# A Griffin-style layer in fp32: u, gelu, q and k by seven half-size products too, the recurrent branch spread over them, attention moved beside the recurrent projection

## The chip, the cores and the metric

One core of one Trainium2 chip runs the whole program. The metric is device time in microseconds of one execution; the median of 3 runs before is 1458.74 us (1458.58 to 1458.85).

## The reference, cut to what matters

The layer works on 1024 tokens of width 1024 in fp32. One input projection gives seven parts of each token; an attention branch and a recurrent branch use them and meet before the output projection, then a feed-forward block follows.

```python
h = rms_norm(x, ln1_g)
z = h @ w_in + b_in
q, k, v, u, y, g_att, g_rec = split(z)      # widths 512 512 512 1024 1024 1024 1024
y_att = neighbourhood_attention(q, k, v, rpb) @ w_att_o
u = centred_depthwise_conv(u, conv_w, conv_b)
h_fwd = rg_lru(u, ..., reverse=False)       # two sigmoid gates, then a scan along the tokens
h_bwd = rg_lru(u, ..., reverse=True)
y_rec = ((h_fwd + h_bwd) * gelu(y)) @ w_rec_o
x = x + (sigmoid(g_att) * y_att + sigmoid(g_rec) * y_rec) @ w_out
x = x + square(relu(rms_norm(x, ln2_g) @ w_ff1)) @ w_ff2
return rms_norm(x, lnf_g)
```

## The kernel before, in words

Every fp32 operand of a matrix product is split into a high and a low part of type fp32r, and a product is three matmuls: high by high, high by low, low by high. A matmul takes a 128x128 block of weights and 512 columns (tokens).

The program is written once as a list of operations and ordered by a planner. `M(fn)` (line 379) puts a unit of usually six matmuls on TensorE's main list; `SD(pos, fn, boost)` (line 383) puts side work, on any engine, at a position counted in such units; `here()` is the current position. `Plan.add` (line 119) gives each operation a cost in ns and its predecessors, `Plan.solve` (line 204) runs a list schedule with these costs and a limited number of tile slots and banks, and `Plan.issue` (line 326) records the instructions in the order of the planned start times. So every instruction of the profile has line L332, and groups are told apart by tile names. Engines run their own instructions strictly in that order. For VectorE (DVE) the cost of an operation without a branch of its own is n/0.96+68 ns for n elements a row, the scan among them: 1135 ns at 1024. PSUM tiles carry the tag "pm" (two of them) or "pa" (four).

The stages, with their times in the trace:

- 0 to 76 us: norm, transposes, the v part; 76 to 218 us: the 2048 gate columns in eight **pairs** (`pairs`, line 634).
- 218 to 404 us: q and k as full products (`tprod`, line 815: 48 matmuls for 128 output columns of weights), with the 64 attention tiles (`a_qk`, `a_norm`, `a_tr`, `a_av`, lines 904 to 943) beside them.
- 404 to 613 us: u and y, eight full products each (`utask`, `ytask`, lines 977 to 988), with the recurrent branch of each of eight channel blocks as side work: convolution (tile uc), split (uh, ul), four gate products on TensorE (`gate_pe`), sigmoids, tanh, exp, square and square root (tiles g, th, sq), two scans (`scan`, line 1074).
- 613 to 658 us: projection of the attention result; 658 to 745 us: projection of the recurrent result (both `tprod`); 745 to 839 us: output projection.
- 839 to 1145 us: first feed-forward product, sixteen pairs by the same `pairs`; 1145 to 1457 us: second feed-forward product.

A pair computes two 128-column blocks of weights against the two token halves by seven half-size products of 12 matmuls each (named A11, A12, A22 and S1 to S4 for the weight side), 84 matmuls in place of 96. `pjob` (line 534) loads both weight tiles (ws), makes sums (sa, sb) on DVE and splits them (wh, wl; sh, sl; wx) on ScalarE (ACT) and DVE. `prod` (line 587) runs one product into a bank of its own, and `ev1` to `ev7` (lines 605 to 632) add the seven results together: one ACT copy and seven DVE additions of 128x512 from PSUM. `gate_store` (line 802) applies the sigmoid and stores the gate in DRAM (gd).

Of the kernel before, what the change touches and what calls it, by code (L numbers as in the profile page):

```python
# [4 lines left out]
F32 = mybir.dt.float32  # L5
# [5 lines left out]
P = 128  # L11
# [3 lines left out]
DH = 64  # L15
# [4 lines left out]
NSLOT = 51  # L20
# [86 lines left out]
class Plan:  # L107
# [11 lines left out]
    def add(self, eng, meth, args, kw):  # L119
# [224 lines left out]
def emit(tc, x, prm, wst, wv, wg, watt, wrec, wout, wff1, wff2, tb, bv, lnf, out):  # L344
# [3 lines left out]
    plan = Plan({"t": NSLOT - NW, "w": NW, "s": 48, "pm": 2, "pa": 4, "c": 64, "d": 72})  # L348
    pe, act, dve, pool, sp = [plan.engine(e) for e in ("pe", "act", "dve", "pool", "sp")]

    with ExitStack() as ctx:
# [182 lines left out]
        def pjob(o, srcs, p0, p1):  # L534
# [15 lines left out]
            def sa():  # L550
                o.sa = T("sa", F32, (P, 8, P))
                dve.tensor_add(o.sa[:, 0:4], o.w1[:, 0:4], o.w1[:, 4:8])
                dve.tensor_sub(o.sa[:, 4:8], o.sa[:, 0:4], o.w0[:, 0:4])

            def sb():
                o.sb = T("sb", F32, (P, 8, P))
                dve.tensor_sub(o.sb[:, 0:4], o.w0[:, 0:4], o.w1[:, 0:4])
                dve.tensor_sub(o.sb[:, 4:8], o.w0[:, 4:8], o.sa[:, 4:8])
# [17 lines left out]
            SD(p1 - 20, lambda: dma(1))  # L576
            SD(p1 - 6.8, sa, 6.0)
            SD(p1 - 6.7, lambda: sp_("sa", "ha", "la"), 6.0)
            SD(p1 - 3.2, sb, 6.0)
            SD(p1 - 1.5, lambda: sp_("sb", "hb", "lb"), 6.0)  # L580
            SD(p1 - 0.5, a22, 6.0)
            o.lhs = {"A11": lambda: (o.h0[:, 0:4], o.l0[:, 0:4]), "A12": lambda: (o.h0[:, 4:8], o.l0[:, 4:8]),
                     "S1": lambda: (o.ha[:, 0:4], o.la[:, 0:4]), "S2": lambda: (o.ha[:, 4:8], o.la[:, 4:8]),
                     "S3": lambda: (o.hb[:, 0:4], o.lb[:, 0:4]), "S4": lambda: (o.hb[:, 4:8], o.lb[:, 4:8]),
                     "A22": lambda: (o.a4[:, 0:4], o.a4[:, 4:8])}

        def prod(o, a, ob, b, bank, ev, boost=5.0):

            h = Obj()
            for kk in range(2):  # L590
                def run(kk=kk):
                    if kk == 0:
                        h.ps = VT(nm("pm"), (P, 512), F32, "pm") if bank else PA()
                    hi, lo = o.lhs[a]()
                    for k in (2 * kk, 2 * kk + 1):
                        bh, bl = ob[b]["h"][kk][:, k % 2, :], ob[b]["l"][kk][:, k % 2, :]
                        pe.matmul(h.ps, hi[:, k, :], bh, start=(k == 0), stop=False)
                        pe.matmul(h.ps, hi[:, k, :], bl, start=False, stop=False)
                        pe.matmul(h.ps, lo[:, k, :], bh, start=False, stop=(k == 3))
                last = M(run)  # L600
            SD(last + 0.1, lambda: ev(o, h.ps), boost)

        lft, rgt = slice(0, 512), slice(512, 1024)

        def ev1(o, ps):
            o.r1 = T("r1")
            act.activation(o.r1[:, lft], ps, AF.Copy)

        def ev2(o, ps):
            if o.r0 is None:  # L610
                o.r0 = T("r0")
            dve.tensor_add(o.r0[:, lft], ps, o.r1[:, lft])

        def ev6(o, ps):
            if o.r0 is None:
                o.r0 = T("r0")
            dve.tensor_add(o.r0[:, rgt], ps, o.r1[:, lft])

        def ev7(o, ps):
            dve.tensor_add(o.r1[:, rgt], ps, o.r0[:, rgt])  # L620

        def ev4(o, ps):
            dve.tensor_add(o.r1[:, lft], ps, o.r1[:, rgt])

        def ev5(o, ps):
            dve.tensor_add(o.r0[:, rgt], ps, o.r0[:, rgt])
            dve.tensor_add(o.r1[:, rgt], ps, o.r1[:, rgt])
            o.store(o.r1, 1)

        def ev3(o, ps):  # L630
            dve.tensor_add(o.r0[:, rgt], ps, o.r0[:, rgt])
            o.store(o.r0, 0)

        def pairs(srcs, stores, ob, pre):

            ps_ = []
            for st in stores:
                o = Obj()
                o.r0, o.store = None, st
                ps_.append(o)  # L640
# [3 lines left out]
            for i0 in range(0, pre, 2):  # L644
                g = ps_[i0:min(i0 + 2, pre)]
                for o in g:
                    prod(o, "A11", ob, "B11", 1, ev1, 30.0)
                for o in g:
                    prod(o, "A12", ob, "B21", 1, ev2, 30.0)
            for i, o in enumerate(ps_):  # L650
                if i >= pre:
                    pjob(o, srcs[i], here(), here() + 2)
                    prod(o, "A11", ob, "B11", 1, ev1, 10.0)
                prod(o, "S2", ob, "T2", 0, ev6)
                if i >= pre:
                    prod(o, "A12", ob, "B21", 1, ev2)
                prod(o, "S3", ob, "T3", 0, ev7)
                prod(o, "A22", ob, "T4", 0, ev4)
                prod(o, "S1", ob, "T1", 0, ev5)
                prod(o, "S4", ob, "B22", 0, ev3)  # L660
# [130 lines left out]
        V = [[None, None] for _ in range(4)]  # L791

        def gather_v(g):
            for b in range(2):
                V[g][b] = T("V", F32, (P, 2, 512))
            for b in range(2):
                sp.dma_start(V[g][b], vd[g][2 * b:2 * b + 2].rearrange("n p f -> p n f"))


        gd = [None] * 16  # L800

        def gate_store(i):
            def store(r, half):
                c = 2 * i + half
                act.activation(r, r, AF.Sigmoid, bias=col("bga" if c < 8 else "bgr", c % 8), scale=1.0)
                gd[c] = Dr("gd")
                sp.dma_start(gd[c], r)
            return store

        pairs([(wst[24 + 2 * i], wst[25 + 2 * i]) for i in range(8)], [gate_store(i) for i in range(8)], ob1, PRE1)  # L810
        for g in range(4):
            SD(here() - 4 + 3 * g, lambda g=g: gather_v(g))
# [24 lines left out]
        qs, kh, kl = [None] * 4, [None] * 4, [None] * 4  # L837
        QL, KL = (5.0, 7.0), (0.2, 1.4)
        att, attd = [None] * 4, [None] * 4
        kend = []  # L840
        for m in range(4):
            w = wjob(wst[m], (P, 8, P), here())
            o = tprod(w, hT)

            qs[m] = [None, None]

            def evq(m=m, o=o):
                o.t = T("q")
                for hf in range(2):
                    c = slice(hf * 512, (hf + 1) * 512)  # L850
                    act.activation(o.t[:, c].rearrange("p (n r c) -> p r n c", r=8, c=16),
                                   o.ps[:, c].rearrange("p (r n c) -> p r n c", n=4, c=16),
                                   AF.Identity, bias=bq8[:, m:m + 1], scale=0.125)

            def stq(hd, m=m, o=o):
                qs[m][hd] = t = T("qs", F32R)
                a, b = slice(hd * DH, (hd + 1) * DH), slice((1 - hd) * DH, (2 - hd) * DH)
                act.activation(t[a], o.t[a], AF.Copy)
                dve.tensor_sub(t[b], o.t[a], t[a])
            SD(o.last + 0.1, evq, 30.0)  # L860
            for hd in range(2):
                SD(o.last + QL[hd], lambda hd=hd, f=stq: f(hd))
            w = wjob(wst[4 + m], (P, 8, P), here())
            o = tprod(w, hT)
            kh[m], kl[m] = [None, None], [None, None]

            def evk(m=m, o=o):
                o.t = T("k")
                act.activation(o.t, o.ps, AF.Identity, bias=col("bk", m), scale=1.0)

            def stk(hd, m=m, o=o):
                kh[m][hd] = h = T("kh", F32R)
                kl[m][hd] = l = T("kl", F32R)
                a, b = slice(hd * DH, (hd + 1) * DH), slice((1 - hd) * DH, (2 - hd) * DH)
                act.activation(h[a], o.t[a], AF.Copy)
                act.activation(h[b], o.t[a], AF.Copy)
                dve.tensor_sub(l[a], o.t[a], h[a])
                dve.tensor_sub(l[b], o.t[a], h[a])
            SD(o.last + 0.1, evk, 30.0)
            for hd in range(2):  # L880
                SD(o.last + KL[hd], lambda hd=hd, f=stk: f(hd))
            kend.append(o.last)
        SD(kend[0] - 12, softplus)

# [711 lines left out]
```

## Time and profile before

| what | value |
|---|---|
| median of 3 runs | 1458.74 us |
| profiled execution, its own time | 1459.04 us |
| its span, first to last instruction | 1457.3 us |
| instructions | 17684 |
| PE, DVE, ACT busy | 1434.7, 1061.3, 739.1 us |
| granted TensorE clock | 0.999 |
| HBM traffic | 133 GB/s over the span |

The span leaves 1.74 us of the profiled execution around it. A busy share is that of an engine's instructions over the whole span. Rows give a start (timeline and chain) or a sum and a mean (groups); a start-to-start distance on one engine is up to 0.1 us shorter than the durations, since an instruction begins while the one before ends.

### The profile page before, as it was taken

What the parts mean: (1) busy time and instruction counts of PE and PEld (TensorE: products, weight loads), DVE (VectorE), ACT (ScalarE), POOL (GpSimd) and SP (SyncE); (2) the same over time, 40 slices, a digit from 0 to 9 for tenths busy, and PEclk for the clock granted to TensorE, in tenths of its full rate; (3) what the DMA queues carried; (4) which work ended last, traced back from release to release, by engine and by line L of the source; (5) the groups of instructions that cost most, each with busy time, mean ns of one, the idle gap of its engine ahead of it and who ended that gap; (6) DMA issues with size and microseconds to landing.
All of it is one profiled execution on the core that took longest, in us unless ns stands there. A gap on an engine that the chain in (4) does not pass through costs nothing.

```text
span 1457.3 us, 17684 instructions
## 1 busy us (share of the span) xinstructions
PE 1434.7 (98%) x6688; PEld 1178.1 (81%) x6688; DVE 1061.3 (73%) x1601; ACT 739.1 (51%) x1146; POOL 0.7 (0%) x6
## 2 busy tenths in 40 slices
PE   6999999999999999999999999999999999999997
PEld 5888888778778887888888888888888888888886
DVE  6985645666859899975444589776766976866996
ACT  7743325665576987941225545444443643432454
POOL 0000000000000000000000000000000000000000
PEclk9999999999999999999999999999999999999999
DMA  6532235233311013422323325544446884336312
GB/s 226 150 119 101 102 136 209 94 127 113 109 39 63 30 52 108 156 94 98 130 86 116 122 95 185 175 147 142 152 152 234 311 318 148 113 115 235 117 43 101
DMA packets 71445, 195.47 MB, mean 134 GB/s; under 512 B 7360, under 2 KB 7488, under 8 KB 71360
## 3 DMA queue, kind: packets, MB, share of 16 engines
q1 hardware_dynamic: 71360, 194.35, 38.8%
q8 instruction: 52, 0.85, 0.2%
q14 instruction: 33, 0.27, 0.1%
HBM read 141.89 MB, written 52.43 MB: 133 GB/s over the span
## 4 chain that ended last, share of the span: by engine, by line
PE 88%; DVE 8%; issue 1%; ACT 1%; DMA 1%; SPq 0%; DVEq 0%
PE pa L332 57%; PE pm L332 32%; DVE g L332 3%; DVE wl L332 1%; DVE uc L332 1%; DVE wh L332 1%; DVE y L332 1%; DMA x<-in_x_dram 0%; DVE th L332 0%; ACT h L332 0%; DMA ws<-in_wst_dram 0%; DVE al L332 0%; ACT L332 0%; DVE uh L332 0%; DVE h L332 0%
## 5 line engine op out<-in xcount | busy, mean ns | idle before, releaser
L332 PE MATMUL pa<-wh,rh 128*128 128x512 f32 x448 | 173.9, 389 | 0.0
L332 PE MATMUL pa<-wl,rh 128*128 128x512 f32 x448 | 173.5, 389 | 0.0
L332 PE MATMUL pa<-wh,rl 128*128 128x512 f32 x448 | 172.8, 389 | 0.0
L332 DVE TENSOR_TENSOR r<-pa,r 128x512 f32<-128x512 f32 x144 | 96.9, 688 | 77.0 <-PE pa L332 76.6
L332 PE MATMUL pm<-hTh,wh 128*128 128x512 f32 x448 | 148.5, 399 | 0.0
L332 PE MATMUL pm<-hTl,wh 128*128 128x512 f32 x448 | 146.1, 392 | 0.0
L332 PE MATMUL pm<-hTh,wl 128*128 128x512 f32 x448 | 144.5, 390 | 0.0
L332 DVE TENSOR_TENSOR wl<-ws,wh 128x1024 fp32r<-128x1024 f32 x76 | 92.4, 1221 | 20.5 <-PE pm L332 12.8
L332 ACT ACTIVATE wh<-ws 128x1024 fp32r<-128x1024 f32 x49 | 51.4, 1057 | 105.6 <-DMA ws<-in_wff_dram 58.2
L332 ACT ACTIVATE wh<-w 128x1024 fp32r<-128x1024 f32 x56 | 58.9, 1051 | 88.0 <-PE pa L332 77.8
L332 PEld LDWEIGHTS pm<-hTh,wl 128*128 128x128 f32 x448 | 84.0, 188 | 17.7
L332 PEld LDWEIGHTS pa<-wl,rh 128*128 128x128 f32 x448 | 84.1, 188 | 17.6
L332 PEld LDWEIGHTS pa<-wh,rh 128*128 128x128 f32 x448 | 84.1, 188 | 17.5
L332 PEld LDWEIGHTS pa<-wh,rl 128*128 128x128 f32 x448 | 84.1, 188 | 17.4
L332 PEld LDWEIGHTS pm<-hTl,wh 128*128 128x128 f32 x448 | 83.7, 188 | 17.8 <-issue 0.7
L332 ACT ACTIVATE r<-r 128x1024 f32<-128x1024 f32 x64 | 67.0, 1059 | 59.4 <-DVE r L332 58.9
L332 PEld LDWEIGHTS pm<-hTh,wh 128*128 128x128 f32 x448 | 81.0, 188 | 18.2 <-issue 4.1
L332 ACT ACTIVATE rh<-rs 128x1024 fp32r<-128x1024 f32 x56 | 58.7, 1049 | 42.7 <-DVE wl L332 17.3
L332 DVE TENSOR_TENSOR acc<-pa,acc 128x512 f32<-128x512 f32 x72 | 49.3, 688 | 41.3 <-PE pa L332 41.1
L332 DVE TENSOR_TENSOR wl<-w,wh 128x1024 fp32r<-128x1024 f32 x56 | 68.2, 1219 | 10.6 <-ACT wh L332 9.6
L332 DVE TENSOR_TENSOR rl<-rs,rh 128x1024 fp32r<-128x1024 f32 x56 | 68.2, 1219 | 8.8 <-ACT rh L332 7.9
L332 PE MATMUL pa<-T4h,wx 128*128 128x512 f32 x192 | 63.0, 389 | 0.0
(205 smaller groups left out, 3217.6 us busy)
## 6 DMA issues: line engine op xcount, KB each, us to landing
rs<-rd SPq DMA_DIRECT2D x56, 512.0 KB, 7.2
ws<-in_wst_dram SPq DMA_DIRECT2D x41, 512.0 KB, 4.5
ws<-in_wff_dram SPq DMA_DIRECT2D x36, 512.0 KB, 5.1
w<-in_wff_dram SPq DMA_DIRECT2D x32, 512.0 KB, 6.8
B<-in_tb_dram SPq DMA_DIRECT2D x32, 384.0 KB, 3.7
x<-in_x_dram SPq DMA_DIRECT2D x16, 512.0 KB, 6.4
gd<-r SPq DMA_DIRECT2D x16, 512.0 KB, 2.9
g<-gd SPq DMA_DIRECT2D x16, 512.0 KB, 4.5
```

The source lines that it names most:

```text
L332: getattr(eng[op.eng], op.meth)(*[r(a) for a in op.args], **{k: r(a) for k, a in op.kw.items()})
```

## The change: what it does

- u, y, q and k go through `pairs` as well: with the gates there are 20 pairs in one stretch, in the order of the table PORD.
- The products of a pair are chained in PSUM: A11, S2, S3 and A22 add up in one bank (tag pm), S1 and S4 in another, A12 has its own. Partial sums are read out between (ev1, ev6, ev5 and ev4 as ACT copies; ev2, ev7 and ev3 as DVE additions): four ACT copies and three DVE additions.
- The weight sums are made in place in the ws tiles; weights are loaded 16 and 15 units ahead instead of 22 and 20.
- The recurrent branch hangs on the ends of the u pairs (RSTEP 28, RRATE 1.6). y, q, k, the recurrent result and its projection go through DRAM (yd, qd, kd, recd, yrd).
- The recurrent projection comes before the attention projection, with the attention tiles beside it (AOFF 3, ASTEP 0.8). V is gathered per pair of heads.
- The sigmoid of the 2048 gates becomes 0.5(1+tanh(z/2)), taken beside the two projections, with the factor 0.5 in `wo_ev`.
- The first operation of the convolution, the split of uc and high parts of weights move from DVE to ACT.
- The planner's costs for TensorE change; three tile slots more (51 to 54), with a smaller DMA scratch.

```diff
-NSLOT = 51
+NSLOT = 54
...
-            op.cost = (n * 0.84 if meth == "transpose" else (52 if wr[0].box[0][0] else n * 1.68) if f32 else n * 0.417) + 2.6
+            op.cost = n * 0.84 + 2.6 if meth == "transpose" else (12 if wr[0].box[0][0] else n * 1.68 + 40) if f32 else n * 0.417 + 13.3
...
+            def sums():
+                a, b = o.w0, o.w1
+                o.a4 = VT(nm("wx"), (P, 8, P), F32R, "w")
+                act.activation(o.a4[:, 0:4], b[:, 4:8], AF.Copy)
+                dve.tensor_sub(o.a4[:, 4:8], b[:, 4:8], o.a4[:, 0:4])
+                dve.tensor_add(b[:, 4:8], b[:, 0:4], b[:, 4:8])
+                dve.tensor_sub(b[:, 0:4], a[:, 0:4], b[:, 0:4])
+                dve.tensor_sub(a[:, 0:4], b[:, 4:8], a[:, 0:4])
+                dve.tensor_sub(a[:, 4:8], a[:, 4:8], a[:, 0:4])
...
-            SD(p0 - 22, lambda: dma(0))
+            SD(p0 - 16, lambda: dma(0))
...
-        def prod(o, a, ob, b, bank, ev, boost=5.0):
+        def prod(o, a, ob, b, key, bank, first, ev, boost=5.0):
...
-                    if kk == 0:
-                        h.ps = VT(nm("pm"), (P, 512), F32, "pm") if bank else PA()
+                    if kk == 0 and first:
+                        o.ps[key] = VT(nm("pm"), (P, 512), F32, "pm") if bank else PA()
...
+                    prod(o, "A11", ob, "B11", 0, True, True, ev1, 10.0)
+                    prod(o, "A12", ob, "B21", 1, False, True, ev2)
+                prod(o, "S2", ob, "T2", 0, False, False, ev6)
+                prod(o, "S1", ob, "T1", 2, False, True, ev5)
+                prod(o, "S3", ob, "T3", 0, False, False, ev7)
+                prod(o, "S4", ob, "B22", 2, False, False, ev3)
+                prod(o, "A22", ob, "T4", 0, False, False, ev4)
...
+        PORD = (("u", 0), ("y", 0), ("g", 0), ("u", 1), ("y", 1), ("g", 1), ("g", 2), ("u", 2), ("y", 2), ("g", 3),
+                ("g", 4), ("u", 3), ("y", 3), ("g", 5), ("g", 6), ("g", 7), ("qk", 0), ("qk", 1), ("qk", 2), ("qk", 3))
...
+        RSTEP, RRATE, AOFF, ASTEP = 28.0, 1.6, 3.0, 0.8
...
+            base = end_of["u", j // 2] + 0.3 + (j % 2) * RSTEP
...
+        pos0 = [RO + AOFF + 16 * ASTEP * m for m in range(4)]
...
-            dve.tensor_add(x1[t][:, cs], o.ps, x1[t][:, cs])
+            dve.scalar_tensor_tensor(x1[t][:, cs], o.ps, 0.5, x1[t][:, cs], ALU.mult, ALU.add)
```

How the rows of the programs change at the places of which the prediction speaks (a number behind a name tells tiles of that name apart; a SCALAR_TENSOR_TENSOR g<-g,g is a scan):

On DVE before, in the recurrent stretch, two scans of one channel block stand together, behind them the weight parts of the next products:

```order
L332 TENSOR_TENSOR g_917_4384<-g_917_4384,th_927_4436 128x1024
L332 TENSOR_TENSOR g_925_4426<-g_925_4426,th_929_4446 128x1024
L332 SCALAR_TENSOR_TENSOR g_917_4384<-g_914_4355,g_917_4384 128x1024
L332 SCALAR_TENSOR_TENSOR g_925_4426<-g_922_4410,g_925_4426 128x1024
L332 TENSOR_TENSOR g_947_4543<-g_947_4543,uc_935_4381 128x1024
L332 TENSOR_TENSOR wl_958_4564<-ws_943_4491,wh_956_4514 128x1024
```

On DVE in the change, at the first such place in the stretch of pairs, the two scans stand between the addition that reads bank pa_281 (ev3 of a pair) and the low parts of the weights of the next pairs (wl, sl):

```order
L332 TENSOR_TENSOR r0_270_1595<-pa_281_1657,r0_270_1595 128x512
L332 TENSOR_TENSOR g_257_1522<-g_257_1522,th_271_1585 128x1024
L332 TENSOR_TENSOR g_267_1568<-g_267_1568,th_272_1606 128x1024
L332 SCALAR_TENSOR_TENSOR g_257_1522<-g_251_1481,g_257_1522 128x1024
L332 TENSOR_TENSOR sl_297_1774<-ws_258_1535,sh_296_1761 128x1024
L332 SCALAR_TENSOR_TENSOR g_267_1568<-g_261_1548,g_267_1568 128x1024
L332 TENSOR_TENSOR g_295_1780<-g_295_1780,uc_268_1556 128x1024
L332 TENSOR_TENSOR wl_313_1800<-ws_300_1754,wh_312_1789 128x1024
```

So eviction, scans and weight parts of a pair share one queue within a few instructions; TensorE issues 32 matmuls between the last one into pa_281 and the first that reads wl_313.

On ACT in the change, late in the stretch, the copies out of PSUM stand among the splits and the recurrent block's functions; bank pm_573 is read three times, each time with more products added up in it:

```order
L332 ACTIVATE r0_576_3436<-pm_573_3413 128x512
L332 ACTIVATE wh_579_3441<-ws_568_3403 128x1024
L332 ACTIVATE sq_578_3448<-g_560_3363 128x1024
L332 ACT_TABLE_LOAD
L332 ACTIVATE th_566_3385<-th_566_3385 128x1024
L332 ACTIVATE wx_585_3469<-ws_575_3432 128x512
L332 ACTIVATE th_567_3393<-th_567_3393 128x1024
L332 ACTIVATE r0_576_3436<-pm_573_3413 128x512
L332 ACTIVATE r1_583_3495<-pa_582_3477 128x512
L332 ACTIVATE sh_591_3509<-ws_575_3432 128x1024
L332 ACTIVATE sh_586_3528<-ws_568_3403 128x1024
L332 ACTIVATE r1_583_3495<-pm_573_3413 128x512
```

Before, ACT read one bank of a pair once, and TensorE never added to a bank after it was read.

## Rows read from the trace of the kernel before

**Rows 1.** The page: busy time and share by engine; the chain that ended last, by engine.
```profile
PE 1434.7 (98%) x6688; PEld 1178.1 (81%) x6688; DVE 1061.3 (73%) x1601; ACT 739.1 (51%) x1146; POOL 0.7 (0%) x6
PE 88%; DVE 8%; issue 1%; ACT 1%; DMA 1%; SPq 0%; DVEq 0%
```
**Rows 2.** Chain of waits, pieces: start us, length us, engine, tile, instructions.
```profile
103.64 2.72 PE pm L332 x12
106.36 2.72 PE pa L332 x12
...
1134.42 315.57 PE pa L332 x1392
```
**Rows 3.** Busy time by stage: length; PE, PEld, DVE, ACT, POOL; clock; DMA share; GB/s.
```profile
76.00:218.00 142.00, 142.00 (x628) 117.60 (x628) 86.20 (x120) 48.63 (x52) 0.00 (x0) 1.00 0.32 113
218.00:404.00 186.00, 186.00 (x1121) 148.11 (x1119) 126.46 (x328) 109.86 (x229) 0.00 (x0) 1.00 0.37 128
404.00:613.00 209.00, 207.01 (x927) 168.44 (x926) 183.21 (x166) 168.03 (x187) 0.00 (x0) 1.00 0.21 68
613.00:658.00 45.00, 44.47 (x197) 36.51 (x196) 37.65 (x33) 22.97 (x23) 0.00 (x0) 1.00 0.38 130
658.00:745.00 87.00, 87.00 (x386) 72.06 (x385) 39.87 (x41) 15.90 (x22) 0.00 (x0) 1.00 0.36 127
```
**Rows 4.** Waits of TensorE: tile waited for, us in total, times, longest.
```profile
PE pa L332 <- DVE uh L332: 1.5, 4, 0.5
PE pm L332 <- DVE wl L332: 0.7, 1, 0.7
```
**Rows 5.** DVE groups by form: busy us, mean ns of one, idle before.
```profile
L332 DVE TENSOR_TENSOR r<-pa,r 128x512 f32<-128x512 f32 x144 | 96.9, 688 | 77.0 <-PE pa L332 76.6
L332 DVE TENSOR_TENSOR wl<-ws,wh 128x1024 fp32r<-128x1024 f32 x76 | 92.4, 1221 | 20.5 <-PE pm L332 12.8 <-issue 6.0 <-ACT wh L332 1.2
L332 DVE TENSOR_TENSOR_SCAN g<-g,g 128x1024 f32<-128x1024 f32 x16 | 36.4, 2284 | 0.1
```
**Rows 6.** Timeline of DVE, two stretches: start us, us, instruction.
```profile
60.16 0.69 DVE L332 TENSOR_TENSOR v<-pm,bvb 128x512 f32<-128x512 f32 x1
60.76 0.69 DVE L332 TENSOR_TENSOR F<-F,F 128x512 f32<-128x512 f32 x1
...
464.52 2.29 DVE L332 TENSOR_TENSOR_SCAN g<-g,g 128x1024 f32<-128x1024 f32 x1
466.72 0.67 DVE L332 CAST uh<-uc 128x1024 fp32r<-128x1024 f32 x1
467.30 1.22 DVE L332 TENSOR_TENSOR wl<-ws,wh 128x1024 fp32r<-128x1024 f32 x1
468.44 1.23 DVE L332 TENSOR_TENSOR ul<-uc,uh 128x1024 fp32r<-128x1024 f32 x1
```
**Rows 7.** Timeline of PE at the same place; in brackets the idle time before.
```profile
466.71 0.39 PE L332 MATMUL pm<-hTh,wl 128*128 128x512 f32 x1
467.45 1.20 PE L332 MATMUL pa<-uh,wh 128*128 128x512 f32 x4 [0.35 <-DVE uh L332]
```
**Rows 8.** Timeline of ACT, in a gate pair and in the recurrent stretch.
```profile
106.39 0.60 ACT L332 ACTIVATE r<-pm 128x512 f32<-128x512 f32 x1 [0.63 <-PE pm L332]
107.12 1.06 ACT L332 ACTIVATE sh<-sa 128x1024 fp32r<-128x1024 f32 x1
...
474.99 1.28 ACT L332 ACT_TABLE_LOAD   x1
476.28 1.06 ACT L332 ACTIVATE y<-y 128x1024 f32<-128x1024 f32 x1
```
**Rows 9.** DMA issues: KB each, median us from issue to landing.
```profile
ws<-in_wst_dram SPq DMA_DIRECT2D x41, 512.0 KB, 4.5
gd<-r SPq DMA_DIRECT2D x16, 512.0 KB, 2.9
g<-gd SPq DMA_DIRECT2D x16, 512.0 KB, 4.5
```

More of the change, by code (lines that the diff above doesn't have):

```diff
@@ L638, in pairs @@
                 o = Obj()
[L639 removed]
+                o.r0, o.store, o.ps = None, st, {}
                 ps_.append(o)
@@ L788, in emit, with st_u, store @@
                 M(lambda q=q, r_=r_: r_(q))
[L791 to L802, printed above, removed]
+        gd, yd, us = [None] * 16, [None] * 8, [None] * 8
+        qd, kd = [None] * 4, [None] * 4
+        def st_u(i):
+            def store(r, half):
+                us[2 * i + half] = r
+            return store
@@ L803, in store, with st_y @@
+        def st_y(i):
             def store(r, half):
                 c = 2 * i + half
-                act.activation(r, r, AF.Sigmoid, bias=col("bga" if c < 8 else "bgr", c % 8), scale=1.0)
-                gd[c] = Dr("gd")
-                sp.dma_start(gd[c], r)
-            return store
-        pairs([(wst[24 + 2 * i], wst[25 + 2 * i]) for i in range(8)], [gate_store(i) for i in range(8)], ob1, PRE1)
-        for g in range(4):
-            SD(here() - 4 + 3 * g, lambda g=g: gather_v(g))
+                act.activation(r, r, AF.Gelu_apprx_tanh, bias=col("by", c), scale=1.0)
+                yd[c] = Dr("yd")
+                sp.dma_start(yd[c], r)
+            return store
@@ new lines, in st_g, with store, st_qk @@
+        def st_g(i):
+            def store(r, half):
+                gd[2 * i + half] = Dr("gd")
+                sp.dma_start(gd[2 * i + half], r)
+            return store
+        def st_qk(m):
+            def store(r, half):
+                if half == 1:
+                    act.activation(r, r, AF.Identity, bias=col("bk", m), scale=1.0)
+                    kd[m] = Dr("kd")
+                    sp.dma_start(kd[m], r)
+                    return
+                t = T("q")
+                for hf in range(2):
+                    c = slice(hf * 512, (hf + 1) * 512)
+                    act.activation(t[:, c].rearrange("p (n r c) -> p r n c", r=8, c=16),
+                                   r[:, c].rearrange("p (r n c) -> p r n c", n=4, c=16),
+                                   AF.Identity, bias=bq8[:, m:m + 1], scale=0.125)
+                qd[m] = Dr("qd")
+                sp.dma_start(qd[m], t)
+            return store
@@ new lines, in emit @@
+        PORD = (("u", 0), ("y", 0), ("g", 0), ("u", 1), ("y", 1), ("g", 1), ("g", 2), ("u", 2), ("y", 2), ("g", 3),
+                ("g", 4), ("u", 3), ("y", 3), ("g", 5), ("g", 6), ("g", 7), ("qk", 0), ("qk", 1), ("qk", 2), ("qk", 3))
+        FIRST = {"u": 8, "y": 16, "g": 24}
+        STORE = {"u": st_u, "y": st_y, "g": st_g, "qk": st_qk}
+        RSTEP, RRATE, AOFF, ASTEP = 28.0, 1.6, 3.0, 0.8
+        B0 = here()
+        ends = pairs([(wst[i], wst[4 + i]) if k == "qk" else (wst[FIRST[k] + 2 * i], wst[FIRST[k] + 2 * i + 1])
+                      for k, i in PORD], [STORE[k](i) for k, i in PORD], ob1, PRE1)
@@ L815, in tprod @@
+        end_of = dict(zip(PORD, ends))
         def tprod(w, objs, kk=KD, wsel=None):
@@ new lines, in stk, with gather_v @@
+        def stk(m, hd, o):
+            kh[m], kl[m] = kh[m] or [None, None], kl[m] or [None, None]
+            kh[m][hd] = h = T("kh", F32R)
+            kl[m][hd] = l = T("kl", F32R)
+            a, b = slice(hd * DH, (hd + 1) * DH), slice((1 - hd) * DH, (2 - hd) * DH)
+            act.activation(h[a], o.k[a], AF.Copy)
+            act.activation(h[b], o.k[a], AF.Copy)
+            dve.tensor_sub(l[a], o.k[a], h[a])
+            dve.tensor_sub(l[b], o.k[a], h[b])
+        def gather_v(m):
+            V[m] = [T("V", F32, (P, 2, 4, P)) for _ in range(2)]
+            for g in range(4):
+                sp.dma_start(V[m][g // 2][:, g % 2], vd[g][:, :, m * P:(m + 1) * P].rearrange("n p f -> p n f"))
@@ L965, in emit @@
             SD(o.pos, lambda o=o: a_qk(o))
-            nxt = [tiles[s + d].pos if s + d < nt else tiles[-1].pos + (s + d - nt + 1) for d in range(4)]
+            nxt = [tiles[s + d].pos if s + d < nt else tiles[-1].pos + (s + d - nt + 1) * ASTEP for d in range(4)]
             SD(nxt[1] + 0.1, lambda o=o: a_norm(o))
@@ L1111, in emit, with rec_load, rec_split @@
-        RE = here()
-        aT = [Obj() for _ in range(4)]
+        rT = [Obj() for _ in range(8)]
+        aT = [Obj() for _ in range(4)]
+        def rec_load(k):
+            rec[k] = T("rec")
+            sp.dma_start(rec[k], recd[k])
+        def rec_split(k):
+            rT[k].hi = T("rh", F32R)
+            rT[k].lo = T("rl", F32R)
+            split(rT[k].hi, rT[k].lo, rec[k])
+        for k in range(8):
+            SD(RO - 16 + 1.2 * k, lambda k=k: rec_load(k))
+            SD(RO - 9 + 1.2 * k, lambda k=k: rec_split(k))
@@ L1138, in emit, with yr_load @@
+        AO = here()
+        mx = Half("mx")
+        SD(AO + 2.05, lambda: mx.alloc(0))
+        SD(AO + 2.06, lambda: mx.alloc(1))
+        def yr_load(j):
+            yr[j] = T("yr")
+            sp.dma_start(yr[j], yrd[j])
+        for k in range(4):
+            SD(AO - 8 + 1.0 * k, lambda k=k: att_load(k))
+            SD(AO - 3.6 + 1.0 * k, lambda k=k: att_split(k))
+        for j in range(8):
             if j % 2 == 0:
-                wa = wjob(watt[j // 2], (P, 2, 4, P), here(), (22.0, 10.3, 10.0), True)
@@ L1160, in emit @@
-        for j in range(8):
-            w = wjob(wrec[j], (P, 8, P), here())
-            SD(here() - 6, lambda j=j: g_load(sg, 8 + j))
-            o = tprod(w, Full(rT))
-            def evyr(o=o, j=j):
-                dve.tensor_mul(sg[j], o.ps, sg[j])
-                dve.tensor_add(mt[j], sg[j], mt[j])
-                for b in range(2):
-                    split(mx.at("h", j, b * 512, 512), mx.at("l", j, b * 512, 512), mt[j][:, b * 512:(b + 1) * 512])
-            SD(o.last + 0.1, evyr, 30.0)
```

402 lines of the change are left out of this document (170 added, 232 removed).

## The prediction, written before the changed kernel was run

> **What bounds the kernel now.** I read first the busy shares and the chain of waits on the page: TensorE is busy 98% of the span and 88% of the chain that ended last is TensorE [rows 1]. So what a change takes from TensorE's instructions counts in full, unless a wait takes its place. Next the price of a matmul, from the chain's pieces in start-to-start time: 12 matmuls of 512 columns take 2.72 us, 1392 take 315.57, both 0.2267 us each [rows 2]. The clock is 1.00 in every stage [rows 3], so one price serves everywhere.
>
> Then the stages [rows 3], since the cover for side work differs between them. Beside the gate pairs (76 to 218 us) DVE is busy 86 of 142 us and ACT 49, and TensorE never waits. Beside q, k and attention it is 126 and 110 of 186, again without a wait. Beside u, y and the recurrent branch it is 183 and 168 of 209, and there TensorE loses 1.99 us, with another 0.53 in the stage behind it: 2.52 in all. The waits name DVE's products, uh above all [rows 4]. In the timelines one such wait can be followed: a scan starts on DVE at 464.52, the split of uc can start only at 466.72, and TensorE, done with its last matmul, begins on uh only at 467.45, 0.35 us late [rows 6, 7]. The planner books 1135 ns for such a scan; the group shows 2284 ns, twice any other 1024-wide operation [rows 5]. Wherever the order puts scans in front of something that TensorE needs, DVE is 1.07 us later per scan than planned (2.2 us from start to start [rows 6], less 1.135). This decides the prediction.
>
> **The change part by part.**
>
> *Removed matmuls.* 24 products of 48 matmuls (8 u, 8 y, 4 q, 4 k; 1152) become 12 pairs of 84 (1008). 144 x 0.2267 = **32.64 us** less, all on the path [rows 1, 2]. The gates' products, the recurrent gate products (192 matmuls), attention and all later stages keep their number.
>
> *Old waits.* The stretch in which the recurrent branch made TensorE wait is gone as such: **-2.52 us** [rows 3].
>
> *Load of the new stretch.* TensorE issues there 20 x 84 + 192 = 1872 matmuls, 424 us. From start to start DVE takes 0.60 us for a 512-wide and 1.14 us for a 1024-wide operation [rows 6]. Per pair: three low parts of 1.14, and one low part of half size, four sums and three additions of 0.60, 8.2 us; x 20 = 164. Per recurrent block: two scans of 2.2 and about twelve 1024-wide operations, 18 us; x 8 = 146. With the recurrent weights some 315 us, 74%. ACT by durations: 1024-wide 1.06, 512-wide out of PSUM 0.60 [rows 8]. Per pair three splits, one of half size and four copies, 6.2 us, x 20 = 124; per recurrent block eight sigmoid pieces and nine 1024-wide functions, 14.4, x 8 = 115; biases, gelu and the q and k stores about 34; 30 table loads of 1.29 from start to start [rows 8], 39. That is some 312 us, 74%. On the average both are lighter than in the old recurrent stretch (88% and 80% [rows 3]). So the average bounds nothing; single places do.
>
> *Places where DVE comes late.* I went along DVE's new order: for each operation that TensorE releases and each later one that TensorE needs, DVE's work between them against TensorE's matmuls between them. The worst place is the one shown above: addition 0.60, two 1.14, scan 2.2, low part 1.14, scan 2.2, two 1.14: 10.7 us, against 32 matmuls, 7.25 us. TensorE waits 3.45 us. Five more places run over, each with just two scans inside: 30.6 us against 131 matmuls (0.9 late), 17.7 against 73 (1.15), 29.5 against 125 (1.2), 18.3 against 73 (1.75) and 11.4 against 48 (0.5). Their sum is 8.95. Each place has two hand-overs between engines; at the wait shown uh ended at 467.39 and TensorE began 0.06 later [rows 6, 7]; I allow 0.1 for each, 1.2 for six places. Together **+10.2 us**. All six would nearly vanish if a scan took what the planner books (2 x 1.07 less at each, 12.8 in all).
>
> *Places where ACT comes late.* Near the third pair a table load and copies, 5.3 us, stand against 20 matmuls, 4.5: **+1.0 us** with the hand-overs. Nowhere else did I find ACT over.
>
> *Chained banks.* This is new: TensorE adds to a bank that has been read. Between the last matmul of one product and the first of the next one in its bank stand 12 matmuls, 2.72 us [rows 2]. A copy that ACT begins at once is over 0.63 us after TensorE (106.36 to 106.99), with a split ahead of it after 1.7, with a table load ahead after 1.9 [rows 2, 8]; on DVE an addition of 0.69 behind a 1024-wide operation takes 1.9 and behind a scan 3.0 [rows 5]. So one operation ahead is covered and a scan is not; those are in the places counted above. Taken at 0 beyond them; bounds 0 and 35 (below).
>
> *Moves.* Attention leaves a stage with 126 us of DVE and 110 of ACT in 186 us for the recurrent projection, 384 matmuls and the 64 tiles (171 us), which had 40 and 16 of 87 for itself [rows 3]. With sums and gate products moved I count DVE at some 112 and ACT at 118 of 171 us: 66% and 69%, near the old 68% and 59%, where nothing waited. The start of the attention projection, its four loads and eight loads of yr behind stores, and the weights of the output projection have 1 to 2 us in hand. **+1.0 us**; ends -1 (TensorE is idle 22.6 us in all [rows 1], nearly all of it at the start and the end, so little more can go) and +4 (two landings of 4.5 us half hidden [rows 9]).
>
> *DMAs.* 64 transfers of 512 KB more on SP's queue (y, q, k, the recurrent result and its projection, out and in). A store lands after 2.9 us, a load after 4.5, weights after 4.5 [rows 9]. Weights are asked for 15 or 16 units of six matmuls ahead, 20 us. Behind a y store and the y load that waits for it some weights still have 10 us. Taken at 0; DMA engines were 21 to 38% busy in these stages [rows 3].
>
> *Sum.* 1459.04 - 32.64 - 2.52 + 10.2 + 1.0 + 1.0 = **1436 us**. This is against the profiled execution, whose span of 1457.3 lies 1.74 us inside it; the median of the runs is 0.3 us lower, which I neglect.
>
> [...] A table load takes 1.28 us and the next function starts 1.29 us after the load's start [rows 8]: nothing lies between. [...]
>
> **The rivals.**
>
> A. *The slack absorbs the scans.* Waits early in the stretch let DVE catch up for all that follows, and the order held the old stretch to 2.52 us although its 16 scans were planned 17 us too short. Then the new waits are again about 2.5 us: 1459.04 - 32.64 - 2.52 + 2.5 - 1 to +1 = **1425 to 1427 us**. For it: the same two scans stand together in the old order. Against it: in the old order 40 us of matmuls belong to each block and few evictions hang on DVE; now each pair has seven.
>
> B. *More waits than counted.* All 16 scans show in full, 17 us; ACT's table loads delay copies at some five places by 1 us; the moves cost 4: 1459.04 - 35.16 + 26 = **1450 us**. For it: ACT has 30 loads of 1.29 us in that stretch, and each copy has a deadline. Against it: ten of the scans then have no cover though DVE is 74% busy.
>
> C. *The chained banks miss their deadline as a rule* and the kernel is **slower**. The queue that decides is ACT's: two 1024-wide splits and a table load ahead of a copy are 3.4 us, 0.63 more for the copy, 4.0 in place of 2.72: TensorE waits 1.3 us. It has the gain of 35.2 us to eat up: 1.76 us in each of the 20 pairs, or 0.98 in each of 36 if the sixteen feed-forward pairs, which take the same code, suffer too. At two such misses per pair it is 1424 + 20 x 2.6 = **1476 us**. For it: three splits and four copies per pair in one queue with the sigmoids; the rows of ACT show sh twice in a row ahead of a copy. Against it: the loads of 74% leave ACT a quarter of the stretch, and beside the feed-forward pairs no recurrent branch runs.
>
> D. *The gain is paid in the attention projection's stretch:* attention beside the recurrent projection comes short by the whole 32 us, time within 3 us of now. That needs a fifth of 171 us lost, at 66 and 69% load; the old rows show none.
>
> E. *Table loads cost twice the row.* Were each of the 30 loads to hold ACT for another 1.29 us, a copy behind one would be over after 0.63 + 2.58 = 3.2 us, past 2.72; at worst all 30 x 1.29 = 39 us reach TensorE, **1475 us**. Against it: 1.29 from load to next function [rows 8].
>
> **How the numbers follow.** My own forecast, 1431 to 1443 us, gets 0.48; A (1423 to 1431) 0.20; B (1443 to 1455) 0.20; D 0.04; C 0.07; E 0.01. The likeliest is **1436 us**. The range takes in A from 1425 on and B to **1450**: 0.48 and some 0.32, **1425 to 1450 us**, 8 in 10. A measurement of this kernel can tell about 0.2% (2.9 us) from no change. Faster by more: 0.88; within: 0.04; slower: 0.08.
>
> **What would show it.** Right: 144 matmuls of 512 columns fewer; waits of TensorE for sl, wl, ul and r named to DVE, 8 to 12 us in all, in windows with two scans; the largest, about 3.5 us, for wl behind the first scans of the second u pair; no wait in the recurrent projection over 1 us. Wrong: waits of TensorE for ACT's copies of the banks in every pair (C); less than 4 us of waits between 76 and 500 us (A); waits for the tiles of the attention in the recurrent projection (D); a clock below 1.00.

## The result, and the profile after

The changed kernel takes 1451.13 us (median of 4 runs, 1450.02 to 1452.04), the one before 1458.72 in the same comparison: ratio 0.9948, 95% interval 0.993 to 0.9965. The gain is real and is 7.6 us, not the 23 that were forecast; the time lies 1.1 us above the range, which ends at rival B's 1450. The profiled execution took 1451.69 us. Of the four executions two, the profiled one among them, had a granted clock of 0.995 and the two others 0.998; these were 1.6 us shorter in the mean, so what the clock costs differs between executions of this kernel.

The page of the changed kernel, busy time by engine and the chain, as [rows 1] has them for the kernel before:

```profile
PE 1413.8 (98%) x6544; PEld 1150.9 (79%) x6544; DVE 1043.6 (72%) x1566; ACT 851.2 (59%) x1321; POOL 0.7 (0%) x6
PE 54%; DVE 4%; ACT 1%; issue 1%; DVEq 0%; ACTq 0%
```

The chain can be followed back only to 592.7 us here and its shares sum to 60%: it says nothing about the stretch in which the time was lost. TensorE issues 144 matmuls fewer (6688 to 6544), as counted. But 144 at 0.2267 us are 32.64 us, and its busy time fell by 20.9 only; its idle time rose from 22.6 to 36.1 us. The question is where 15 us went. The new stages answer it: the stretch of the 20 pairs (first matmul of a pair to the first of the recurrent projection), the recurrent projection with attention, the attention projection; columns as in [rows 3]:

```profile
63.90:517.70 453.80, 437.73 (x1874) 351.25 (x1872) 340.40 (x389) 311.70 (x372) 0.00 (x0) 0.99 0.35 119
517.70:692.00 174.30, 173.87 (x1089) 137.58 (x1088) 122.49 (x306) 115.70 (x238) 0.00 (x0) 1.00 0.61 208
692.00:735.60 43.60, 43.60 (x193) 35.90 (x192) 34.78 (x37) 23.71 (x29) 0.00 (x0) 1.00 0.95 379
```

The two projections have almost nothing to give back (0.43 us idle). The loss sits in the pairs: 1872 matmuls at 0.2267 are 424.4 us, and the stretch takes 453.8. It splits into three parts. The first is idle time of TensorE, 453.80 - 437.73 = 16.07 us; the waits in this stretch by name, with their total, count and longest:

```profile
PE pa L332 <- DVE r L332: 2.9, 2, 2.2
PE pm L332 <- DVE wl L332: 2.6, 1, 2.6
PE pm L332 <- ACT r L332: 1.8, 3, 1.0
PE pa L332 <- ACT uh L332: 1.6, 2, 0.9
PE pm L332 <- DVE r L332: 1.6, 2, 1.4
PE pm L332 <- ACT wh L332: 1.5, 2, 1.1
PE pa L332 <- ACT g L332: 1.0, 1, 1.0
PE pa L332 <- DVE ul L332: 0.9, 2, 0.6
PE pm L332 <- DVE sl L332: 0.8, 1, 0.8
PE pa L332 <- DVE sl L332: 0.7, 1, 0.7
PE pm L332 <- ACT sh L332: 0.5, 1, 0.5
```

These 18 waits sum to 9.5 us for DVE and 6.5 us for ACT. (The longest wait of the run, 9.3 us, is at its start, outside this stretch.)

The second part is the clock. PE's timeline at the longest wait (start, us, instruction):

```profile
187.27 0.39 PE L332 MATMUL pa<-hTh,wl 128*128 128x512 f32 x1
188.15 0.50 PE L332 MATMUL pm<-hTh,wh 128*128 128x512 f32 x1 [0.49 <-ACT wh L332]
188.49 0.40 PE L332 MATMUL pm<-hTl,wh 128*128 128x512 f32 x1
191.51 0.79 PE L332 MATMUL pm<-hTh,wl 128*128 128x512 f32 x1 [2.63 <-DVE wl L332]
192.10 0.63 PE L332 MATMUL pm<-hTh,wh 128*128 128x512 f32 x1
192.53 0.63 PE L332 MATMUL pa<-T1h,sh 128*128 128x512 f32 x1
...
196.80 0.49 PE L332 MATMUL pa<-T1h,sh 128*128 128x512 f32 x1
197.12 0.40 PE L332 MATMUL pa<-T1l,sh 128*128 128x512 f32 x1
```

The granted clock falls within the wait, at 190.2, from 1.00 to 0.50, and is back at 1.00 at 197.0. In that time a matmul takes 0.43 us to the next start instead of 0.227. Thirteen matmuls take 5.61 us instead of 2.95, 2.7 us lost. A second drop to 0.50, from 313.0 to 316.5, follows the second longest wait (2.16 us for r, ended at 312.2) and costs 1.6 us. The two windows in which the clock falls:

```profile
175.00:200.00 25.00, 21.88 (x82) 16.57 (x81) 18.78 (x16) 22.64 (x25) 0.00 (x0) 0.86 0.33 111
300.00:325.00 25.00, 22.84 (x94) 18.41 (x93) 18.26 (x19) 12.00 (x17) 0.00 (x0) 0.93 0.34 116
```

The third part, 437.73 - 424.4 - 4.3 = 9.0 us, counts as busy. A matmul's row lasts 0.39 us though the next one can start after 0.227, so each marked wait is 0.16 us longer than it is marked: 2.9 us for the 18. The first matmul after a wait takes 0.34 us to the next start (188.15 to 188.49), 0.11 more than the others: 2.0 us. Thirteen more hand-overs are late by too little to be marked, and cost 2.6 us in the same two ways. The last 1.5 us are spread in bits over all the other matmuls.

DVE at that place, the one that was worked out ahead:

```profile
183.60 2.28 DVE L332 TENSOR_TENSOR_SCAN g<-g,g 128x1024 f32<-128x1024 f32 x1
185.81 1.20 DVE L332 TENSOR_TENSOR sl<-ws,sh 128x1024 fp32r<-128x1024 f32 x1
186.92 2.28 DVE L332 TENSOR_TENSOR_SCAN g<-g,g 128x1024 f32<-128x1024 f32 x1
189.12 1.20 DVE L332 TENSOR_TENSOR g<-g,uc 128x1024 f32<-128x1024 f32 x1
190.24 1.22 DVE L332 TENSOR_TENSOR wl<-ws,wh 128x1024 fp32r<-128x1024 f32 x1
```

DVE never pauses here; wl, for which TensorE waits from 188.9 to 191.5, comes behind both scans. The forecast was 3.45 us for this place; it is 2.63 by name, and 3.12 with the wait of 0.49 for wh just before it. That one is named to ACT, but ACT had waited for sl, which stands behind the first scan:

```profile
187.04 1.06 ACT L332 ACTIVATE wh<-ws 128x1024 fp32r<-128x1024 f32 x1 [0.25 <-DVE sl L332]
```

### The profile page after: what moved, and what is told of

It is laid out like the page before. It is cut to its first block, busy times and chain, and to the rows that moved or that the text cites. A ratio compares the mean times of both kernels' runs of the same rounds, so it can differ in the third digit from the quotient of the medians.

```text
span 1449.9 us, 17675 instructions
## 1 busy us (share of the span) xinstructions
PE 1413.8 (98%) x6544; PEld 1150.9 (79%) x6544; DVE 1043.6 (72%) x1566; ACT 851.2 (59%) x1321; POOL 0.7 (0%) x6
## 4 chain that ended last, share of the span: by engine, by line
PE 54%; DVE 4%; ACT 1%; issue 1%; DVEq 0%; ACTq 0%
PE pa L332 37%; PE pm L332 17%; DVE acc L332 1%; DVE wl L332 1%; DVE rl L332 1%; ACT fo L332 0%; DVE nu L332 0%; DVE h L332 0%; DVE x L332 0%; ACT h L332 0%; DVE F L332 0%; DVE fo L332 0%; DVE nr L332 0%; DVE T2l L332 0%; ACT wh L332 0%
## 5 line engine op out<-in xcount | busy, mean ns | idle before, releaser
L332 ACT ACTIVATE r<-pm 128x512 f32<-128x512 f32 x102 | 59.9, 588 | 73.9 <-PE pm L332 73.9
L332 DVE TENSOR_TENSOR wl<-ws,wh 128x1024 fp32r<-128x1024 f32 x64 | 77.7, 1220 | 33.9 <-ACT wh L332 33.3
L332 ACT ACTIVATE sh<-ws 128x1024 fp32r<-128x1024 f32 x72 | 75.9, 1059 | 39.3 <-DVE ws L332 39.1
L332 PEld LDWEIGHTS pa<-wh,rl 128*128 128x128 f32 x448 | 84.1, 188 | 17.7 <-DVE rl L332 0.2
L332 PE MATMUL pm<-T4h,wx 128*128 128x512 f32 x272 | 90.0, 391 | 1.7 <-DVE r L332 1.6
L332 DVE TENSOR_TENSOR sl<-ws,sh 128x1024 fp32r<-128x1024 f32 x72 | 87.2, 1217 | 2.7 <-ACT sh L332 2.7
L332 DVE TENSOR_TENSOR r<-pa,r 128x512 f32<-128x512 f32 x74 | 50.7, 685 | 48.1 <-PE pa L332 48.0
L332 ACT ACTIVATE wh<-ws 128x1024 fp32r<-128x1024 f32 x61 | 63.7, 1053 | 12.3 <-DMA ws<-in_wff_dram 4.4
L332 PEld LDWEIGHTS pm<-T4h,wx 128*128 128x128 f32 x272 | 51.0, 188 | 13.6 <-DVE r L332 3.0
L332 PE MATMUL pa<-T1h,sl 128*128 128x512 f32 x144 | 56.6, 393 | 0.7 <-DVE sl L332 0.7
L332 PE MATMUL pa<-T1h,sh 128*128 128x512 f32 x144 | 56.7, 394 | 0.0
```

Source lines behind the costliest of these rows:

```text
L332: getattr(eng[op.eng], op.meth)(*[r(a) for a in op.args], **{k: r(a) for k, a in op.kw.items()})
```

## The experiments

Theory T1: the waits come from DVE, late behind scans that the planner books 1.07 us too short, and the clock drops come from the longest waits. T2: ACT is late of itself (table loads, copies). T3: the chained banks leave too little time whatever the order.

**The planner's cost of a scan corrected, in the changed kernel and in the one before.**

```diff
             aps = sum(1 for a in args[2:] if isinstance(a, VA) and a.free() == 1)
             op.cost = n / (1.92 if two else 0.96) + 68 + 60 * min(aps, 2) if n > 4 else 90
+            if meth == "tensor_tensor_scan":
+                op.cost = 2 * n / 0.96 + 68
```

> Only the planner's cost of a scan is corrected, from 1135 to 2201 ns at 1024 elements; the computation is the same and the order is planned anew. Theory T1 (the new waits are DVE work that comes late behind scans which the planner books 1.07 us too short; the two drops of TensorE's clock follow the two longest of these waits): the waits for DVE in the stretch of pairs fall from 9.5 to under 4 us and the clock stays up, 1436 to 1442 us. Rival T2 (ACT, with its 30 table loads, copies and splits, is what comes late): 1447 to 1452 us, with waits for ACT of 6 us or more. Rival T3 (the chained banks leave evictions too little time whatever the order): 1447 to 1452 us, with waits for r.

> The kernel before with the same corrected scan cost. T1: its waits in the recurrent stretch were only 2.5 us, so it gains 1 to 2.5 us, 1456 to 1458 us, and the seven-product change is worth 16 to 20 us between two kernels that are planned with the right cost. If the cost matters little to any order (against T1): 1458 to 1459.5 us here and no gain in the changed kernel either.

Measured: 1438.61 us (ratio 0.9862, 0.9848 to 0.9877) for the changed kernel, 1456.33 us (0.9984, 0.9974 to 0.9993) for the one before. One line of the planner is worth 12.5 us in the changed kernel and 2.6 in the other (1458.93 in the same comparison), so between kernels planned with the right price the change is worth 17.7 us. The stretch of pairs, the stage behind it, a window inside the stretch, and the waits in the stretch, scan cost corrected:

```profile
64.10:504.50 440.40, 433.40 (x1874) 349.96 (x1873) 340.62 (x389) 310.85 (x372) 0.00 (x0) 1.00 0.35 123
504.50:678.90 174.40, 173.97 (x1090) 137.63 (x1089) 122.55 (x306) 115.72 (x238) 0.00 (x0) 1.00 0.61 209
250.00:275.00 25.00, 22.60 (x88) 16.97 (x87) 21.86 (x22) 13.65 (x19) 0.00 (x0) 0.93 0.19 64
```
```profile
PE pa L334 <- ACT uh L334: 3.0, 2, 2.2
PE pm L334 <- ACT wh L334: 1.3, 2, 1.1
PE pm L334 <- ACT r L334: 1.2, 3, 0.7
PE pa L334 <- DVE sl L334: 0.5, 1, 0.5
PE pa L334 <- DVE ul L334: 0.5, 1, 0.5
```

The stretch is 13.4 us shorter, with DVE as busy as ever (340 us), and the stage behind it is the same to 0.1 us. The time and the waits for DVE (9.5 to 1.1 us) are as T1 expected, and the time is out of reach of T2 and T3. One part of T1 failed: the clock did not stay up. It fell once more, between 250 and 275 us (0.93 in the mean of these 25 us, by an estimate some 3.5 us at 0.50). The same 25 us hold the wait of 2.2 us for uh, and that wait is for ACT. What is left are mostly waits for ACT.

**Scans as plain products, order kept.** The scan is issued as one product of its two operands; the planner's cost and so every engine's order stay.

```diff
+            if op.meth == "tensor_tensor_scan":
+                eng[op.eng].tensor_tensor(*[r(a) for a in op.args[:3]], ALU.mult)
+                continue
```

> The changed kernel, every engine's order kept, but each of the 16 scans is issued as a plain elementwise product of the same 1024 elements, so DVE takes what the planner booked; the recurrence is left out. T1: the waits for DVE fall from 9.5 to under 3 us, the clock stays up, 1437 to 1443 us. T2 or T3: the waits for ACT and for r stay, 1446 to 1451 us.

Measured: 1433.58 us (0.983, 0.9815 to 0.9844), 17.5 us less than the changed kernel and below all that was expected. Sixteen scans are short by 1.07 us each, 17.1 us: **in sum as much reached the end**, as rival B had it, and not only the part that runs over at six places. That the two sums agree so well is partly luck, for they do not agree scan by scan: two of the scans alone give 4.3 us for 2.2 (below). The stretch, and what TensorE still waits for in it (two waits of 0.2 us left out):

```profile
64.60:500.00 435.40, 431.59 (x1874) 348.40 (x1873) 324.05 (x389) 311.82 (x372) 0.00 (x0) 1.00 0.36 124
```
```profile
PE pm L335 <- ACT wh L335: 1.1, 1, 1.1
PE pm L335 <- DVE wl L335: 0.9, 1, 0.9
PE pa L335 <- DVE ul L335: 0.9, 2, 0.6
PE pm L335 <- ACT r L335: 0.5, 2, 0.3
```

DVE's busy time falls by 16.4 us, the clock stays at 1.00 and idle time goes from 16.07 to 3.81 us. The waits for ACT went too, from 6.5 to under 2 us, though nothing of ACT's was changed: most of them had come from DVE's lateness, as the one at 188.15 shown above. The waits for DVE fall from 9.5 to 1.9 us. So of the 18.4 us by which the stretch is shorter, 7.6 are waits for DVE by name, 4.7 waits for ACT, 4.3 the clock, and 1.8 come off the part that counts as busy; 7.2 us of that part stay.

**Table loads away, order kept; then both.**

```diff
+            if op.eng == "act" and op.sets and op.tiles[0].tag == "t" and op.args[0].base.name.split("_")[0] in ("g", "th", "r1", "r0"):
+                op.args[2] = AF.Identity
```

> The changed kernel, order kept, but sigmoid, tanh, exp, square root and gelu of the gate, recurrent and y tiles are issued as identity, so 29 of the 34 table loads go (37 us of ACT); these functions are left out. T1: the waits for DVE behind scans stay, those for ACT (6.5 us) go in part, 1444 to 1449 us. T2: both go, since ACT is what comes late, 1436 to 1442 us. T3: 1447 to 1451 us.

> Both at once, order kept: the 16 scans as plain products and 29 table loads gone (the recurrence, and sigmoid, tanh, exp, square root and gelu are left out). It shows what is left of the waits when neither scans nor tables make an engine late. T1 (scans decide; ACT's lateness is mostly a consequence): 1430 to 1433 us, at most 3.5 us below the run with the scans alone replaced (1433.6). T2 (ACT is late of itself): 1424 to 1429 us. T3 (the chained banks cost of themselves): the waits for r stay and the time is no more than 1 us below 1433.6.

Measured: 1443.18 us (0.9896, 0.9881 to 0.9911) without the tables, 1428.19 us (0.9792, 0.9775 to 0.9808) without tables and with the scans as products. The stretch, first without tables, then with both:

```profile
63.90:508.40 444.50, 433.24 (x1874) 350.00 (x1872) 340.60 (x389) 275.08 (x343) 0.00 (x0) 1.00 0.35 122
```
```profile
64.10:494.20 430.10, 428.18 (x1874) 349.87 (x1873) 324.18 (x389) 274.44 (x343) 0.00 (x0) 1.00 0.36 126
```

Neither expectation of the first run holds: 8.0 us lie between those of T1 and T2. Some of the 37 us of table loads reach the end: 8.0 us while the scans are late too, 5.4 us when they are not (1433.58 - 1428.19, within T2's range of the second run). So T2 is right as a second, smaller cause, and the forecast of 1.0 us for ACT was too low. With both gone TensorE is idle 1.9 us in 430. Without the tables alone, the wait for r that had been 2.16 us is at most 1.4 and the one for wl is still 2.6 us; the clock over the stretch is 1.00, for 0.99 in the changed kernel.

**Only two scans as products, order kept.** The test of the clock.

```diff
+TWO = ("g_257", "g_267")
...
+            if op.meth == "tensor_tensor_scan" and op.args[0].base.name in TWO:
+                eng[op.eng].tensor_tensor(*[r(a) for a in op.args[:3]], ALU.mult)
+                continue
```

> The changed kernel, order kept, but only the two scans at 183.6 and 186.9 us of its trace, ahead of its longest wait (2.63 us for wl, at the start of which TensorE's clock fell to half for 6.8 us), are issued as plain products of the same size; the recurrence of one channel block is left out. Theory T1 with the clock as a cost of its own: that wait shrinks to about 0.5 us, the clock drop there goes (3.4 us), 1444 to 1447.5 us. If the clock drop does not hang on that wait, or costs nothing: only the shorter wait, of which later places take back a part, 1448 to 1450.5 us, with a drop still there.

Measured: 1446.87 us (0.9919, 0.9904 to 0.9934), 4.3 us less for 2.2 us less of DVE work, in the range of T1. The two windows again, in this run:

```profile
175.00:200.00 25.00, 23.97 (x101) 18.17 (x100) 17.09 (x17) 24.27 (x28) 0.00 (x0) 1.00 0.31 117
300.00:325.00 25.00, 22.85 (x94) 18.43 (x93) 18.09 (x20) 13.46 (x19) 0.00 (x0) 0.93 0.34 119
```

The wait for wl there is 0.9 us, the clock stays up, and the second drop is still where it was. So the first drop hung on the late scans before that wait. It had cost 2.7 of the 3.65 us that lie between the two profiled executions (1451.69 and 1448.04). The 14 other scans, 15.0 us of excess, were worth the rest of the 17.5 us, 13.3.

**The chained banks alone, in the kernel before.** `pjob`, `prod`, `ev1` to `ev7` and `pairs` of the change put into the kernel before, for its gates and the feed-forward product.

```diff
-                prod(o, "S2", ob, "T2", 0, ev6)
...
-                prod(o, "S4", ob, "B22", 0, ev3)
...
+                prod(o, "S2", ob, "T2", 0, False, False, ev6)
...
+                prod(o, "A22", ob, "T4", 0, False, False, ev4)
```

> The kernel before with one part of the change alone: the eight gate pairs and the sixteen feed-forward pairs take the chained banks, the new evictions, the sums in place and the shorter lead of the weights; everything else as before. T3 (chained banks leave evictions too little time): slower by 0.3 to 1 us per pair, 1465 to 1480 us. T1 (a chain costs nothing while DVE and ACT are on time): 1457 to 1461 us.

Measured: 1461.39 us (1.0018, 1.0008 to 1.0027). It costs 2.5 us, not 0.3 to 1 us per pair, in single waits where a run of pairs begins:

```profile
PE pm L332 <- DVE sl L332: 1.1, 1, 1.1
PE pm L332 <- ACT r L332: 0.5, 1, 0.5
```

T3 (rival C) falls: while DVE and ACT are on time, a bank that is read between its products costs next to nothing. The last version below bears it out in the new stretch, with 20 chained pairs and one marked wait. Whether the chains make lateness dearer there was not tried.

**Versions that go further.** With the corrected scan cost, the recurrent blocks start later after their pair; then their sigmoids are taken by tanh, for which 27 table loads stand in the program in place of 35 (in the changed kernel the gates' tanh and the attention's exponentials stand together behind one load, at 526.87 us); then the spacings and the leads of three weight splits are moved again. Each version is ordered anew.

```diff
-        RSTEP, RRATE, AOFF, ASTEP = 28.0, 1.6, 3.0, 0.8
+        RSTEP, RRATE, AOFF, ASTEP = 25.0, 1.6, 3.0, 0.8
...
-            base = end_of["u", j // 2] + 0.3 + (j % 2) * RSTEP
+            base = end_of["u", j // 2] + 4.0 + (j % 2) * RSTEP
```

> The changed kernel with the scan's cost corrected, and each recurrent block starting 4 units (of six matmuls) after the end of its u pair instead of 0.3, the second block of a pair 25 units later instead of 28. If the remaining waits (about 9 us between 75 and 450 us in the run with the corrected cost alone, most of them for uh and wh of ACT) come from the first operations of a recurrent block falling on the end of its pair: 1431 to 1435 us. If they come from the load as such: 1437 to 1441 us.

```diff
-                    act.activation(g[:, b * 512:(b + 1) * 512], pss[b], AF.Sigmoid,
-                                   bias=col("ba" if ty == 0 else "bi", d * 8 + j), scale=1.0)
+                    act.activation(g[:, b * 512:(b + 1) * 512], pss[b], AF.Tanh,
+                                   bias=bab5[:, ty * 16 + d * 8 + j:ty * 16 + d * 8 + j + 1], scale=0.5)
...
```

> As the run with the later recurrent blocks (1431.5 us), and the recurrent gates' sigmoids are taken as 0.5(1+tanh(z/2)), so that they share a table with the exponentials: 27 table loads in place of 35, some 10 us less of ACT. If ACT's own lateness is part of what is left (the order-kept run with scans and tables gone was 5.4 us below the one with the scans alone): 1427 to 1430.5 us. If the planner's corrected order already hides the tables: 1430.5 to 1433 us.

```diff
-        RSTEP, RRATE, AOFF, ASTEP = 25.0, 1.6, 3.0, 0.8
+        RSTEP, RRATE, AOFF, ASTEP = 22.0, 1.7, 3.0, 0.8
...
-            base = end_of["u", j // 2] + 4.0 + (j % 2) * RSTEP
+            base = end_of["u", j // 2] + 8.0 + (j % 2) * RSTEP
...
-            SD(p0 - 9.3, lambda: a1(0), 8.0)
+            SD(p0 - 11.0, lambda: a1(0), 8.0)
...
-            SD(p1 - 2.7, lambda: sp_("w1", "hb", "lb"), 6.0)
+            SD(p1 - 4.4, lambda: sp_("w1", "hb", "lb"), 6.0)
```

> The same with the recurrent blocks 8 units after their pair and 22 units apart (rate 1.7), and the first weight split of a pair 1.7 units earlier: 24 table loads. If the start of the recurrent blocks among the pairs still matters: 1426 to 1429.5 us; if what is left is small waits of the switch between tiles: 1429.5 to 1432 us, no better than the run beside it.

Measured: 1431.51 us (0.9813, 0.9798 to 0.9828), 1429.3 us (0.9799, 0.978 to 0.9819) and **1426.82 us** (0.9782, 0.9768 to 0.9797). All three fall into the first of their two expectations: where the recurrent blocks start among the pairs matters, and so do the tables. The last version moves the blocks and the splits together, so its 2.5 us are not parted between them. The last one's stretch, and the only wait that is marked in it:

```profile
64.40:492.90 428.50, 426.95 (x1874) 350.59 (x1873) 341.55 (x390) 300.47 (x362) 0.00 (x0) 1.00 0.36 126
```
```profile
PE pm L334 <- ACT wh L334: 1.3, 1, 1.3
```

DVE is as busy as in the changed kernel (341.6 and 340.4 us) in a stretch 25.3 us shorter. So on DVE the order made the difference, not the load; on ACT there are 10 table loads fewer as well (24 for 34). This version beats both kernels, by 31.6 and 24.3 us.

## Why the prediction was wrong

- *Removed matmuls, 32.64 us:* right in number and price. The attention projection behind the pairs bears the price out: 192 matmuls take 43.6 us.
- *Old waits, -2.52:* right; the corrected scan cost alone gives the kernel before 2.6 us.
- *Load of the stretch:* right in the sum. DVE is busy 340 us by durations (315 was counted from start to start), ACT 312 (312). The reading of it failed: 75% busy was read as room. The old recurrent stretch had 88% and lost 2 us; the new one is lighter and lost 29. That TensorE now needs DVE within a few us more often is the likely reason; no run tests it by itself.
- *Places where DVE comes late, +10.2:* **this step failed**, not in its mechanism but in its price. With the scans at the planned length the stretch is 18.4 us shorter and the kernel 17.5. The sum counted only the time by which DVE runs over its cover at six places. By name the waits for DVE are 9.5 us, of which the scans make 7.6, and the largest is at the place forecast, with 2.6 to 3.1 us for 3.45; the five others are not named closely enough to be matched. What it left out is what a late scan starts elsewhere: waits for ACT that had waited for DVE (4.7 us), the two clock drops (4.3) and time that counts as busy (1.8). The term "all 16 scans show in full" stood in rival B, at 17 us, and was set aside because "ten of the scans then have no cover". By the prediction's own count two scans lie in each of the six places, twelve in all, so that only four were left.
- *Places where ACT comes late, +1.0:* too small as well. 6.5 us by name, most of it DVE's; the table loads alone cost 5.4 us of the kernel's time with the scans out of the way, 8.0 with them late.
- *The clock:* put at nothing without a reason, 4.3 us in the profiled execution. "A clock below 1.00" stood among the signs of being wrong, but no term of the sum allowed for it.
- *Hand-overs:* 1.2 us were allowed for twelve of them. Without late scans and without the tables the stretch still takes 5.7 us more than its matmuls, 1.9 of it idle.
- *Chained banks, 0:* nearly right, 2.5 us for 24 pairs measured alone.
- *Moves, +1.0 and DMAs, 0:* they cost no more than that. Recurrent projection with attention: 0.43 us idle in 174.3; no wait of TensorE in the stretch of pairs names a transfer.

Against the sum: the pairs were forecast at 424.4 + 11.2 = 435.6 us and took 453.8, 18.2 more. By the runs that keep the order, the 29.4 us above the matmuls are 18.4 for the scans (453.8 - 435.4; forecast 10.2), 5.3 for the tables once the scans are short (435.4 - 430.1; forecast 1.0 for ACT) and 5.7 that stay (nothing was put down for them). Everything else came out at 1451.69 - 453.8 = 997.9 us, 2.6 less than the 1000.5 implied.

Rival B had the time (1450) and the right first term, and with ACT at 5 us a good second one. But its 4 us for the moves were not lost, and the 5.7 us that stay were not in it: that its sum fits so closely is luck. Rivals C and D are out by the runs with the chained banks alone and by the rows of the projections, rival A by the waits. Rival E: a table load at 178.31 us of the changed kernel is followed by the next function at 179.60, as before [rows 8]; no time lies between.

ACT's timeline there:

```profile
178.31 1.28 ACT L332 ACT_TABLE_LOAD   x1
179.60 2.01 ACT L332 ACTIVATE th<-th 128x1024 f32<-128x1024 f32 x2
```

## What to carry to other kernels

Where a scheduler sets the order, compare its price of each operation with the trace's before anything else: an operation booked too short runs over every time. Here 16 of them, short by 17.1 us in all, cost 17.5 us, on an engine that was 75% busy. Price a lateness by the whole of what it starts (waits of a third engine, a lost clock, a slower matmul at each hand-over), or better by a run that takes the operation's excess away and keeps the order. When a change moves little, correct the planner for the kernel before and the kernel after: the gap between the two is what the change itself is worth.

## What the runs showed of the hardware that was not expected

- TensorE's granted clock fell to 0.50 for 6.8 us in a wait of 2.63 us, and for 3.4 us behind one of 2.16; with the scan cost corrected it was 0.93 in the mean of the 25 us that hold a wait of 2.2. The first drop went when its wait was cut to 0.9 us. Behind the other waits of the changed kernel's stretch, up to 1.36 us (ended at 438.68), the clock stayed at 1.00.
- A matmul that starts late by a wait takes 0.11 us longer to the next start (0.34 instead of 0.227), and a wait is 0.16 us longer than the timeline marks it (a row of 0.39 less 0.227).
- A scan over 1024 elements takes nearly twice a plain product of that size, 2281 and 1219 ns; [rows 5] had shown it, and the planner did not expect it.
- Reading a bank between two products that add up in it, from ACT and from DVE, showed hardly a cost of its own: 2.5 us over 24 pairs, most of it in waits at two beginnings.
